# Bias rows in other banks, casts behind copies, keys ahead of low weights: three changes of order in a two-layer decoder trunk

## The chip, the cores and the metric

The kernel runs on one core of a Trainium2 chip. The metric is the device time of one execution in microseconds, the median over several executions. The core's engines run side by side, each through its own queue of instructions: TensorE (PE) multiplies matrices and transposes, VectorE (DVE) and ScalarE (ACT) work element by element, GpSimd (POOL) does little here, and SyncE (SP) issues the loads. An instruction that waits for a semaphore holds everything behind it in its engine's queue.

## The reference

Two layers on a sequence of 256 tokens with 1024 channels. Layer 0 mixes tokens by three groups of dilated causal window attention with a relative bias, layer 1 by gated linear attention (GLA) in chunks of 64. Each is followed by a gated feed-forward network with a short convolution (FFN). Every sub-layer has a norm in front, modulated by shift, scale and gate, which are linear functions of a conditioning vector `c`. The change lies in layer 0's attention:

```
qkv = (h @ w_in).reshape(B, S, 3 groups, 3, 16 heads, 64)
s = einsum(q * 64**-0.5, k) + bias[bucket(distance)]      # per group, masked to the window
p = exp(s - max(s));  o_g = p @ v / sum(p);  lse_g = max(s) + log(sum(p))
o = sum over groups of softmax(lse)_g * o_g
x = x + g1 * (o @ w_out)
```

All inputs are float32. The output is the final norm of `x`.

## The kernel before

**Products.** Each large product is made of three float32r products: a weight tile comes to SBUF as `raw`, ACT casts it to the high part `whi` (line 187, in layer 0's first stage line 412), DVE subtracts to get the low part `wlo` (line 191, there line 417), and PE adds `hi*hi`, `lo*hi` and `hi*lo` (lines 197 to 199 in `mm3`). Activations are split the same way into `hhi` and `hlo`. `raw` has four buffers, `whi` and `wlo` three each. A load can go out when a `raw` buffer is free, which is when its low part has been made.

**Modulation.** The 48 chunks of `w_ada` come through the same `raw` buffers. DVE multiplies them with `c` and sums (line 160), ACT adds the bias (lines 168 and 170). Eight chunks are used in the first stage, one with each of the eight channel tiles (`dots`); the rest go one after each group's queries (`next_ada`) and later.

**Order.** The program is written as a stream; a scheduler orders each engine's instructions by its own estimate of times. `behind(i)` and the arguments `after`, `low` and `late` place instructions in that order behind others. They are no semaphores: waits come from data and from buffers alone.

**Banks.** PSUM has eight banks, in three pools: `p` has two, `s` four, `t` two. `bank(name, tag)` takes the next of a pool; without a tag the pool comes from a fixed cycle, "pstspsts". A bank can be written again when its last reader is done.

**First stage (lines 353 to 447 and 617 to 650).** The squares of `x` are summed on PE into bank `ms`, and ACT makes the norm's factor. Three products with a one-hot matrix (line 374, `rows`) make the bias rows of all heads, ACT copies them to SBUF (line 433), SP stores them to DRAM, and from there each pair of heads loads its bias tile later. Five products on constants (`keep_warm`) follow. Then the eight channel tiles are taken one by one: load the modulation chunk and the weights (`dots`), scale (`scaled`), add the shift and cast (`shifted`), low part (`rest_of`), cast the weights in two pieces (`cast`), low weights (`low`). PE multiplies each tile for the first two of eight head pairs, all of it into eight banks: `s`, `t`, `t`, `p`, `p` and three more `s`.

**Head pairs (lines 652 to 716).** For each further pair `u`: queries and keys of three groups (`queries`, `wqk`, into a `p` bank, evacuated by `evacuate`: ACT's `q` at line 546, DVE's `k` at line 547), values in two halves (`values`, `wv`, into the two `p` banks, copied by ACT in `by_group`), scores (`s` banks), maxima and softmax. The probabilities of the pair before are transposed four tiles at a time (`turn`: PE line 518, ACT's copy to `pt` at line 519) and multiplied with the values (`outputs`: PE lines 526 and 530, then `ohi`, `olo`). The third pair (`u == 2`) is special: two earlier pairs are finished in it. The last (`u == 7`) takes its second half of values after the scores. In `project` the last pair is transposed and finished between the output projection's products.

Of the kernel before, what the change touches and what calls it, by code (L numbers as in the profile page):

```python
# [36 lines left out]
KEYS = T + 2 * CH  # L37
# [20 lines left out]
def trunk(ctx: ExitStack, tc: tile.TileContext, I, out):  # L58
    nc = tc.nc
# [12 lines left out]
    def bank(name="ps", tag=None):  # L72
        tag = tag or next(cycle)
        return psum.tile([P, 512], F32, tag=tag, name=name, bufs={"p": 2, "s": 4, "t": 2}[tag])
# [45 lines left out]
    @contextmanager  # L120
    def behind(*those):

        with ExitStack() as st:
            for i in those:
                st.enter_context(tc.issue_after(i.ins))
            yield

    def keep_warm(n):

        ps = bank("warm")  # L130
        for i in range(n):
            i = mm(ps[:, :P], ones_d, ones_d, start=True, stop=True)
        return i
# [3 lines left out]
    sq = wspl.tile([P, 2048], F32, tag="wlo", name="sq").rearrange("p (k t) -> p k t", k=KT)  # L137
    for n in range(2):
        ps = bank("cb", "t")
# [37 lines left out]
    def split(src, n, dmas=1, after=((), ()), late=(), low=()):  # L177
        raw = wraw.tile([P, 2048], F32, tag="raw", name="raw")
        for i in range(dmas):
            c = slice(n * i // dmas, n * (i + 1) // dmas)  # L180
            last_load[0] = nc.sync.dma_start(raw[:, c], src[:, c])
        hi = wspl.tile([P, 2048], F32R, tag="whi", name="whi")
        lo = wspl.tile([P, 2048], F32R, tag="wlo", name="wlo")
        for i in range(0, n, n // 2):
            c = slice(i, i + n // 2)
            with behind(*after[i > 0]):
                copied[0] = nc.scalar.copy(hi[:, c], raw[:, c])  # L187
        for i in range(0, n, n // 2):
            c = slice(i, i + n // 2)
            with behind(*(late if i else low)):  # L190
                last_lo[0] = nc.vector.tensor_tensor(lo[:, c], raw[:, c], hi[:, c].bitcast(F32), op=ALU.subtract)  # L191
        return hi, lo
# [13 lines left out]
    def rstd_of(squares, n=D, tag=None):  # L206
        ps = bank("ms", tag)
        for i, sq in enumerate(squares):
            a = mm(ps[:, :T], ones_d, sq, start=(i == 0), stop=(i == len(squares) - 1))
        ln = tmp.tile([P, T], F32, tag="ln", name="ln", bufs=2)  # L210
        nc.scalar.activation(ln, ps[:, :T], AF.Ln, bias=eps[:, 0:1], scale=D / n)
        r = tmp.tile([P, T], F32, tag="rstd", name="rstd", bufs=2)
        norm_ops[:] = a, nc.scalar.activation(r, ln, AF.Exp, scale=-0.5)
        return r
# [125 lines left out]
    rows = att.tile([16, NROW], F32, tag="pt", name="rows")  # L340
# [22 lines left out]
    with behind(last_add):  # L363
        on_dve = [scale_terms(0)]
    exp_ln_after(silu)
    r = rstd_of([sq[:, 0, :], sq[:, 4, :]])

    rows_ps, at = [], 0
    with behind(norm_ops[0]):
        for i, (g, n) in enumerate(ROWS):  # L370
            c = slice(at, at + n)
            ps = bank("rows", "tts"[i])[:16, 0:n]
            rows_ps.append((ps, c))
            last_row = mm(ps, tab[:, 16 * g : 16 * g + 16], oh[:33, c], start=True, stop=True)
            at += n
    with behind(last_row):
        warm = keep_warm(5)
# [3 lines left out]
    on_act = [norm_ops[1]]  # L381
# [16 lines left out]
    def shifted(kt):  # L398
        with behind(on_act[0]):
            on_act[0] = nc.scalar.activation(h_hi[kt][:, :], xr[kt], AF.Identity, bias=mod[0, 0, kt][:, 0:1])  # L400

    def rest_of(kt):
        with behind(on_dve[0]):
            on_dve[0] = nc.vector.scalar_tensor_tensor(h_lo[kt][:, :], xr[kt], mod[0, 0, kt][:, 0:1], h_hi[kt][:, :].bitcast(F32),
                                                       op0=ALU.add, op1=ALU.subtract)
        chain[kt] = chain[7] = on_act[0], on_dve[0]
        h.append((h_hi[kt], h_lo[kt]))

    def cast(kt, half):
        c = pieces[half]  # L410
        with behind(on_act[0]):
            on_act[0] = nc.scalar.copy(w0[kt][0][:, c], raw0[kt][:, c])

    def low(kt, half):
        c = pieces[half]
        with behind(on_dve[0]):
            on_dve[0] = nc.vector.tensor_tensor(w0[kt][1][:, c], raw0[kt][:, c], w0[kt][0][:, c].bitcast(F32), op=ALU.subtract)
# [2 lines left out]
    scaled(0)  # L420
    cast(0, 0)
    shifted(0)
    cast(0, 1)
    rest_of(0)
    low(0, 0)
    dots(1)
    low(0, 1)
    scaled(1)
    shifted(1)
    rest_of(1)  # L430
    with behind(on_act[0]):
        for ps, c in rows_ps:
            on_act[0] = nc.scalar.copy(rows[:, c], ps)
    for kt in range(2, KT):
        for half in range(2):
            cast(kt - 1, half)
# [58 lines left out]
    def probabilities(prob, m):  # L495
# [14 lines left out]
                normed_p.append(pn)  # L510
        return normed_p, att.tile([P, 4, KEYS], F32, tag="pt", name="pt")

    def turn(tiles, normed_p, pt):
        for i in tiles:
            t = bank("t", "ttss"[i])
            for j in range(3):
                c = slice(P * j, P * j + P)
                last = nc.tensor.transpose(t[:, c], normed_p[i][:, c], ident)
            nc.scalar.copy(pt[:, i, :], t[:, 0:KEYS])
        return last  # L520

    def outputs(u, v, pt):
# [18 lines left out]
    def evacuate(q, k, g, pq, pk):  # L541

        if g:
            i = nc.scalar.mul(q[g], pq, 0.125)
            return i, nc.vector.tensor_copy(k[g], pk)
        qh, ql = q[0]
        pk = in_order(pk)
        kh, kl = (as_tokens(z[:, 0:T]) for z in k[0])  # L550
        nc.scalar.mul(qh, pq, 0.125)
        i = nc.scalar.copy(kh, pk)
        nc.vector.scalar_tensor_tensor(ql, pq, 0.125, qh.bitcast(F32), op0=ALU.mult, op1=ALU.subtract)
        return i, nc.vector.tensor_tensor(kl, pk, kh.bitcast(F32), op=ALU.subtract)
# [30 lines left out]
        return end  # L585

    def queries(u, g, *qk):
        pq, pk, middle, end = raw_queries(u, g)
        with behind(evacuate(*qk, g, pq, pk)[1]):
            next_ada()  # L590
        return middle, end

    def raw_queries(u, g, tag="p", low=(), by_parts=False):
        w = split(I["wqk"][u - 2, g], 2048, low=low, late=low)
        pqk = bank("pqk", tag)
        pq, pk = pqk[:, :T], pqk[:, T:]
        if by_parts:
            for part in range(3):
                for kt in range(KT):
                    for i, ps in enumerate((pq, pk)):  # L600
                        at = 2 * P * kt + P * i
                        end = mm(ps, w[part == 2][:, at : at + P], h[kt][part == 1], start=(part == kt == i == 0),
                                 stop=(part == 2 and kt == KT - 1 and i == 1))
            return pq, pk, None, end
        for kt in range(KT):
            s, e = kt == 0, kt == KT - 1
            mm3(pq, parts(w, 2 * P * kt), h[kt], s, False)
            end = mm3(pk, parts(w, 2 * P * kt + P), h[kt], False, e)
            if kt == 3:
                middle = end  # L610
        return pq, pk, middle, end
# [13 lines left out]
    pv = b0[3:]  # L625
# [37 lines left out]
    qk = new_qk()  # L663
# [14 lines left out]
    for u in range(2, NPAIR):  # L678
        if u > 2:
            bias = bias_of(u)  # L680
            qk = new_qk()
        with behind(last):
            if u > 2:
                queries(u, 0, *qk)
            middle, end = queries(u, 1, *qk)
        if u == 2:
            bias = bias_of(u)
            with tc.issue_after(last_load[0].ins):
                nc.sync.dma_start(x_all, I["xT"])
        with behind(middle):  # L690
            turn((0, 1), *before)
        with behind(end):
            turned = turn((2, 3), *before)
        if u == 2:
            turned_pt, before = before[1], probabilities(*raised)
        middle, end = queries(u, 2, *qk)
        if u == 2:
            with behind(end):
                outputs(0, v0, turned_pt)
                turn((0, 1), *before)  # L700
        pv = [bank("pv", "p") for _ in range(2)]
        end = values(u, 0, pv)
        if u == 2:
            with behind(end):
                turned = turn((2, 3), *before)
        if u < NPAIR - 1:
            end = values(u, 1, pv)
        with behind(end, turned):
            s, last = scores(*qk)
        with behind(last):  # L710
            last = outputs(u - 1, v, before[1])
        if u == NPAIR - 1:
            with behind(last):
                values(u, 1, pv)
        v = by_groups(pv)
        before = probabilities(*maxima(s, bias))

# [543 lines left out]
```

## Time and profile before

| | us |
|---|---|
| median of 3 runs | 778.48 (778.16 to 780.02) |
| the profiled execution's own time | 778.91 |
| its span, first to last instruction | 777.1 |
| PE busy | 757.8 (98%) |
| DVE busy | 625.5 (80%) |
| ACT busy | 490.7 (63%) |

The granted clock of TensorE was 0.998 over the span. A row of the timeline is: start, duration, engine, line, operation, out<-in, form and count, and in brackets the idle time of that engine just before and what ended it. `SPq` is the load queue. In the waits a row is: engine and work that waited, what it waited for, microseconds in all, times, the longest. Durations of PE's products overlap, so the distance from one start to the next is what a product costs: in the first stage six products of 128x256 take 0.71 us.

### The profile page before, as it was taken

Reading aid. Unit: us, or ns where it says so; the run is one execution under the profiler, and the core shown is the slowest. Engines: PE = TensorE matmul, PEld = TensorE weight load, DVE = VectorE, ACT = ScalarE, POOL = GpSimd, SP = SyncE. Lnnn points to the kernel's source line nnn. Section 1 sums busy time; section 2 is a strip of 40 time slices with the busy share of each in tenths; the row PEclk is TensorE's granted clock in tenths of the full one; section 3 lists DMA queues with packets and bytes.
Section 4 is the critical chain, followed back from the end, with each engine's and each line's share of the span. In section 5 each row is a group of like instructions: output and inputs, shape, how many; then the busy total and the mean of one; then the engine's idle time right before and its main releaser. Section 6 shows DMA issues by size and latency. Waiting matters only on the chain.

```text
span 777.1 us, 15925 instructions
## 1 busy us (share of the span) xinstructions
PE 757.8 (98%) x6420; PEld 731.9 (94%) x6420; DVE 625.5 (80%) x1120; ACT 490.7 (63%) x964; POOL 12.4 (2%) x36
## 2 busy tenths in 40 slices
PE   5999999999999999999999999999999999999997
PEld 2999889999999989999999998898999999999997
DVE  6976978778778868999988778797667998899662
ACT  5555765655666668767666556836667876667552
POOL 0000000000000010000000000000010000000000
PEclk9999999999999999999999999999999999999999
DMA  9987787686886846867646975875245665555641
GB/s 344 400 302 286 214 325 262 226 306 212 311 328 245 313 153 243 278 224 257 233 144 236 341 276 200 324 270 217 84 167 184 219 218 179 202 193 207 242 172 55
DMA packets 36487, 186.29 MB, mean 240 GB/s; under 512 B 8444, under 2 KB 11004, under 8 KB 20286
## 3 DMA queue, kind: packets, MB, share of 16 engines
q1 hardware_dynamic: 36032, 184.84, 66.7%
q8 instruction: 50, 0.82, 0.4%
q10 hardware_dynamic: 382, 0.45, 0.2%
q14 instruction: 23, 0.19, 0.1%
HBM read 184.17 MB, written 1.10 MB: 238 GB/s over the span
## 4 chain that ended last, share of the span: by engine, by line
PE 71%; DMA 13%; DVE 11%; ACT 3%; issue 2%; SPq 0%; DVEq 0%; ACTq 0%
PE pab L199 10%; PE pab L198 10%; PE pab L197 10%; DMA raw<-in_wqk 7%; PE pd L197 5%; PE pd L199 5%; PE pd L198 5%; DVE wlo L191 5%; PE pqk L641 4%; DMA raw<-in_wv 4%; DVE ada_raw L160 2%; PE py L197 2%; PE py L198 2%; PE py L199 2%; ACT whi L187 2%
## 5 line engine op out<-in xcount | busy, mean ns | idle before, releaser
L191 DVE TENSOR_TENSOR wlo<-raw,whi 128x1024 fp32r<-128x1024 f32 (+2 forms) x258 | 273.7, 1094 | 56.6 <-ACT whi L187 55.9
L187 ACT CAST whi<-raw 128x1024 fp32r<-128x1024 f32 (+2 forms) x258 | 230.5, 942 | 115.8 <-PE pab L198 40.7
L199 PE MATMUL pab<-hhi,wlo 128*128 128x256 f32 x672 | 185.1, 277 | 0.0
L198 PE MATMUL pab<-hlo,whi 128*128 128x256 f32 x672 | 185.0, 277 | 0.0
L197 PE MATMUL pab<-hhi,whi 128*128 128x256 f32 x672 | 183.5, 277 | 0.0
L199 PEld LDWEIGHTS pab<-hhi,wlo 128*128 128x128 f32 x672 | 126.3, 188 | 0.0
L198 PEld LDWEIGHTS pab<-hlo,whi 128*128 128x128 f32 x672 | 126.1, 188 | 0.2
L197 PEld LDWEIGHTS pab<-hhi,whi 128*128 128x128 f32 x672 | 125.3, 188 | 0.1
L160 DVE CUSTOM_DVE_ANT_0 ada_raw<-ada_raw,c_bc 128x1024 f32<-128x1024 f32 x96 | 113.6, 1222 | 14.3 <-DMA ada_raw<-in_w_ada 14.3
L198 PE MATMUL pd<-glo,whi 128*128 128x256 f32 x352 | 97.1, 276 | 0.0
L199 PE MATMUL pd<-ghi,wlo 128*128 128x256 f32 x352 | 97.1, 276 | 0.0
L197 PE MATMUL pd<-ghi,whi 128*128 128x256 f32 x352 | 96.8, 276 | 0.0
L197 PE MATMUL pqk<-hhi,whi 128*128 128x256 f32 x328 | 92.4, 282 | 0.0
L199 PE MATMUL pqk<-hhi,wlo 128*128 128x256 f32 x328 | 91.3, 279 | 0.0
L198 PE MATMUL pqk<-hlo,whi 128*128 128x256 f32 x328 | 91.1, 278 | 0.0
L198 PEld LDWEIGHTS pd<-glo,whi 128*128 128x128 f32 x352 | 66.1, 188 | 0.0
L199 PEld LDWEIGHTS pd<-ghi,wlo 128*128 128x128 f32 x352 | 66.1, 188 | 0.0
L197 PEld LDWEIGHTS pd<-ghi,whi 128*128 128x128 f32 x352 | 65.9, 188 | 0.0
L197 PEld LDWEIGHTS pqk<-hhi,whi 128*128 128x128 f32 x328 | 61.8, 188 | 0.5
L199 PEld LDWEIGHTS pqk<-hhi,wlo 128*128 128x128 f32 x328 | 61.7, 188 | 0.3 <-issue 0.3
L198 PEld LDWEIGHTS pqk<-hlo,whi 128*128 128x128 f32 x328 | 61.7, 188 | 0.0
L822 ACT ACTIVATE r<-pab,small 128x256 f32<-128x256 f32 x86 | 46.7, 559 | 15.7 <-DVE r L825 15.6
(226 smaller groups left out, 1389.6 us busy)
## 6 DMA issues: line engine op xcount, KB each, us to landing
ada_raw<-in_w_ada SPq DMA_DIRECT2D x46, 1024.0 KB, 5.8
raw<-in_w_up SPq DMA_DIRECT2D x42, 1024.0 KB, 5.0
raw<-in_w_down SPq DMA_DIRECT2D x32, 704.0 KB, 5.2
raw<-in_wqk SPq DMA_DIRECT2D x18, 1024.0 KB, 7.7
raw<-in_wv SPq DMA_DIRECT2D x14, 768.0 KB, 4.7
raw<-in_w SPq DMA_DIRECT2D x6, 960.0 KB, 5.7
raw<-in_w_out_a SPq DMA_DIRECT2D x4, 1024.0 KB, 7.1
raw<-in_w_v_b SPq DMA_DIRECT2D x4, 1024.0 KB, 5.8
```

Source lines behind the costliest of these rows:

```text
L160: last_dot[0] = nc.vector.tensor_tensor_reduce(w, w, c_bc, op0=ALU.mult, op1=ALU.add, scale=1.0, scalar=0.0, accum_out=dot,)
L187: copied[0] = nc.scalar.copy(hi[:, c], raw[:, c])
L191: last_lo[0] = nc.vector.tensor_tensor(lo[:, c], raw[:, c], hi[:, c].bitcast(F32), op=ALU.subtract)
L197: mm(ps, a[0], b[0], start=start, stop=False)
L198: mm(ps, a[0], b[1], start=False, stop=False)
L199: return mm(ps, a[1], b[0], start=False, stop=stop)
L641: i = mm(ps[j], w[:, at + P * j : at + P * j + P], y, start=s and j % 2 == 0, stop=e and j % 2 == 1)
L822: nc.scalar.activation(r, u[:, :T], AF.Identity, scale=cw[2], bias=col(C_CB + 44 * l + f))
```

## The change

Three parts and what follows from them.

1. *Bias rows.* The three banks of `rows` are taken from `s` instead of `t`, `t`, `s`. ACT copies them behind the first tile's casts, ahead of the second tile's work, instead of behind the second tile's shift. The banks of `keep_warm` and of the first norm come from `p` and no longer from the cycle, so the cycle's later takers get the pool that stands three places before the old one. The first tile's low weights go ahead of its low activations.
2. *Third pair.* The casts of its values' two halves, and of the next pair's first queries, are placed behind copies of transposed tiles (`first`, `second`, `pt_copy`).
3. *Last pair.* The low parts of the second half of its values are placed behind the copy of its last keys (`kept`).

```diff
     def keep_warm(n):
-        ps = bank("warm")
+        ps = bank("warm", "p")
...
-    r = rstd_of([sq[:, 0, :], sq[:, 4, :]])
+    r = rstd_of([sq[:, 0, :], sq[:, 4, :]], tag="p")
...
-            ps = bank("rows", "tts"[i])[:16, 0:n]
+            ps = bank("rows", "s")[:16, 0:n]
...
+    low(0, 0)
+    rest_of(0)
     cast(0, 1)
-    rest_of(0)
-    low(0, 0)
+    with behind(on_act[0]):
+        for ps, c in rows_ps:
+            on_act[0] = nc.scalar.copy(rows[:, c], ps)
     dots(1)
...
-    with behind(on_act[0]):
-        for ps, c in rows_ps:
-            on_act[0] = nc.scalar.copy(rows[:, c], ps)
...
+    pt_copy, kept = [None], [None, None]
...
-            nc.scalar.copy(pt[:, i, :], t[:, 0:KEYS])
+            pt_copy[0] = nc.scalar.copy(pt[:, i, :], t[:, 0:KEYS])
...
-        pq, pk, middle, end = raw_queries(u, g)
-        with behind(evacuate(*qk, g, pq, pk)[1]):
+        pq, pk, middle, end = raw_queries(u, g, after=pt_copy[:1] if (u, g) == (3, 0) else ())
+        kept[:] = evacuate(*qk, g, pq, pk)
+        with behind(kept[1]):
             next_ada()
...
-        w = split(I["wqk"][u - 2, g], 2048, low=low, late=low)
+        w = split(I["wqk"][u - 2, g], 2048, low=low, late=low, after=(after, after))
...
             turned = turn((2, 3), *before)
+        first = pt_copy[:1] if u == 2 else ()
...
                 turn((0, 1), *before)
+        second = pt_copy[:1] if u == 2 else ()
         pv = [bank("pv", "p") for _ in range(2)]
-        end = values(u, 0, pv)
+        end = values(u, 0, pv, after=first)
...
-            end = values(u, 1, pv)
+            end = values(u, 1, pv, after=second)
...
         if u == NPAIR - 1:
             with behind(last):
-                values(u, 1, pv)
+                values(u, 1, pv, low=kept[1:])
```

**Where the rows stand now.** ACT in the first stage, from the first tile's casts on (`hhi` is the cast activation, `mod` a modulation term). Before:

```order
L412 CAST whi<-raw 128x768
L400 ACTIVATE hhi<-xr,mod 128x256
L412 CAST whi<-raw 128x1152
L170 ACTIVATE mod<-dot,small 128x1
L168 ACTIVATE mod<-dot,one_b,small 128x1
L400 ACTIVATE hhi<-xr,mod 128x256
L433 COPY rows<-rows 16x512
L433 COPY rows<-rows 16x128 x2
L412 CAST whi<-raw 128x768
```

Now:

```order
L412 CAST whi<-raw 128x768
L400 ACTIVATE hhi<-xr,mod 128x256
L412 CAST whi<-raw 128x1152
L428 COPY rows<-rows 16x512
L428 COPY rows<-rows 16x128 x2
L170 ACTIVATE mod<-dot,small 128x1
L168 ACTIVATE mod<-dot,one_b,small 128x1
L400 ACTIVATE hhi<-xr,mod 128x256
L412 CAST whi<-raw 128x768
```

The three copies moved ahead of the second tile's modulation terms and activation.

ACT in the third pair, from its middle queries on (`q` is the copy of queries, 768 columns a half of the values, 1024 a half of queries and keys, `ohi` the outputs' high part). Before:

```order
L187 CAST whi<-raw 128x768 x2
L546 ACTIVATE q<-pqk 128x256
L519 COPY pt<-t 128x384 x3
L187 CAST whi<-raw 128x768 x2
L519 COPY pt<-t 128x384
L170 ACTIVATE mod<-dot,small 128x1
L546 ACTIVATE q<-pqk 128x256
L170 ACTIVATE mod<-dot,small 128x1
L187 CAST whi<-raw 128x1024 x2
L535 CAST ohi<-po 128x256
L519 COPY pt<-t 128x384
L170 ACTIVATE mod<-dot,small 128x1 x2
```

Now:

```order
L548 ACTIVATE q<-pqk 128x256
L521 COPY pt<-t 128x384 x4
L187 CAST whi<-raw 128x768 x2
L170 ACTIVATE mod<-dot,small 128x1 x2
L548 ACTIVATE q<-pqk 128x256
L537 CAST ohi<-po 128x256
L521 COPY pt<-t 128x384
L170 ACTIVATE mod<-dot,small 128x1 x2
L521 COPY pt<-t 128x384
L187 CAST whi<-raw 128x768 x2
L521 COPY pt<-t 128x384 x2
L187 CAST whi<-raw 128x1024 x4
```

Both halves of the values are now cast behind transposed tiles, and two pieces of the fourth pair's queries (four casts) stand together behind the last of them.

DVE in the last pair, from the second group's keys on (`k` is the copy of keys, 768 columns a half of the values). Before:

```order
L547 COPY k<-pqk 128x256
L160 ISA ada_raw,dot<-ada_raw,c_bc 128x1024
L160 ISA dot 128x1
L160 ISA ada_raw,dot<-ada_raw,c_bc 128x1024
L160 ISA dot 128x1
L191 TENSOR_TENSOR wlo<-raw,whi 128x768 x2
L547 COPY k<-pqk 128x256
```

Now:

```order
L549 COPY k<-pqk 128x256
L160 ISA ada_raw,dot<-ada_raw,c_bc 128x1024
L160 ISA dot 128x1
L160 ISA ada_raw,dot<-ada_raw,c_bc 128x1024
L160 ISA dot 128x1
L549 COPY k<-pqk 128x256
L160 ISA ada_raw,dot<-ada_raw,c_bc 128x1024
L160 ISA dot 128x1
L160 ISA ada_raw,dot<-ada_raw,c_bc 128x1024
L160 ISA dot 128x1
L191 TENSOR_TENSOR wlo<-raw,whi 128x768 x2
```

The low weights moved behind the last keys and behind one more modulation chunk.

More of the change, by code (lines that the diff above doesn't have):

```diff
@@ L587, in queries, with raw_queries @@
     def queries(u, g, *qk):
-        pq, pk, middle, end = raw_queries(u, g)
-        with behind(evacuate(*qk, g, pq, pk)[1]):
+        pq, pk, middle, end = raw_queries(u, g, after=pt_copy[:1] if (u, g) == (3, 0) else ())
+        kept[:] = evacuate(*qk, g, pq, pk)
+        with behind(kept[1]):
             next_ada()
         return middle, end
-    def raw_queries(u, g, tag="p", low=(), by_parts=False):
-        w = split(I["wqk"][u - 2, g], 2048, low=low, late=low)
+    def raw_queries(u, g, tag="p", low=(), by_parts=False, after=()):
+        w = split(I["wqk"][u - 2, g], 2048, low=low, late=low, after=(after, after))
         pqk = bank("pqk", tag)
```

## The prediction

> **What bounds the kernel now.** I read the page's first part, then the waits of TensorE (PE), then the timelines of PE, ScalarE (ACT), VectorE (DVE) and the load queue (SP) at the three places that the diff touches.
>
> ```profile
> span 777.1 us, 15925 instructions
> ...
> PE 757.8 (98%) x6420; PEld 731.9 (94%) x6420; DVE 625.5 (80%) x1120; ACT 490.7 (63%) x964; POOL 12.4 (2%) x36
> ```
>
> PE is busy for 98% of the span: 777.1 - 757.8 = 19.3 us of idle time is all that a change of order can win. The list of PE's waits says where it lies (columns: total us, times, longest).
>
> ```profile
> PE warm L132 <- ACT rows L433: 6.4, 1, 6.4
> PE pv L197 <- DVE k L547: 1.4, 1, 1.4
> PE po L526 <- ACT pt L519: 1.3, 1, 1.3
> ...
> PE pv L198 <- DVE wlo L191: 0.6, 1, 0.6
> ...
> PE s L470 <- ACT pt L519: 0.2, 1, 0.2
> ```
>
> The first is the bias rows, the second the last pair's keys, and those that name `pt` (a third one of them, 0.4 us, is quoted below) the third pair. No row names the FFN's banks (`pab`, `pd`).
>
> **The bias rows.** Timeline of the start:
>
> ```profile
> 10.00 2.74 PE L374 MATMUL rows<-oh,tab 33*16 33x512 f32 x6
> ...
> 12.62 1.14 ACT L412 CAST whi<-raw 128x1152 fp32r<-128x1152 f32 x1
> ...
> 15.28 0.29 ACT L170 ACTIVATE mod<-dot,small 128x1 f32<-128x1 f32 x1 [1.52 <-DVE dot L160]
> ...
> 18.51 0.87 ACT L433 COPY rows<-rows 16x512 f32<-16x512 f32 x3
> ...
> 19.12 2.50 PE L132 MATMUL warm<-ones_d 128*128 128x128 f32 x10 [6.38 <-ACT rows L433]
> 19.29 1.88 ACT L412 CAST whi<-raw 128x768 fp32r<-128x768 f32 x2
> ...
> 21.27 0.77 PE L641 MATMUL pqk<-hhi,whi 128*128 128x256 f32 x2
> ```
>
> The five warm-up products take a `t` bank that still holds bias rows; all of PE's queue stands behind them until ACT has copied those rows out, behind tile 1's activation. Now the rows lie in `s` banks, the warm-up in a `p` bank, and nothing of ACT stands before it: it can start at 12.74 (10.00 + 2.74) instead of 19.12, and the first layer's products at 21.27 - 6.38 = 14.9. What they then need is there: the second cast ends at 13.76, and the row copies behind it at 13.76 + 0.87 = 14.6. Those copies cost ACT nothing, as they lie in the 1.52 us in which ACT waited at 15.28; without that cover, 0.87 us of tile 1's chain. They also leave the place ahead of tile 1's casts, which can start at about 18.5 instead of 19.29. The exchange of `low(0, 0)` and `rest_of(0)` on DVE moves instructions that PE needs only after 14.9: nothing.
>
> But PE cannot keep all of it, because casts of later tiles come at their old times. The last tile (kt = 7) decides:
>
> ```profile
> 51.08 1.87 ACT L412 CAST whi<-raw 128x768 fp32r<-128x768 f32 x2
> ...
> 57.81 0.87 PE L641 MATMUL pqk<-hhi,whi 128*128 128x256 f32 x6
> 58.52 0.51 PE L637 MATMUL pqk<-whi,hhi 128*128 128x384 f32 x2
> ...
> 64.16 2.05 PE L602 MATMUL pqk<-hhi,whi 128*128 128x256 f32 x16
> ...
> 40.00:50.00 10.00, 10.00 (x81) 10.00 (x81) 9.10 (x15) 5.09 (x9) 0.00 (x0) 1.00 1.01 392
> ```
>
> (The last row is a window of the stage: after its times PE, weight load, DVE, ACT and GpSimd busy, clock, share of the DMA engines, GB/s.) The DMA engines are full here, so supply is not moved. Tile 7's second cast ends at 51.08 + 1.87 = 52.95; the product that reads it starts at 58.52. PE may come 58.52 - 52.95 = 5.57 us earlier and no more. **I take -5.5.** Upper end 6.38, if the casts come earlier too; lower end 0, in the rival of supply below.
>
> Does the gain survive the next loads?
>
> ```profile
> 63.62 0.60 SPq L353 DMA_DIRECT2D bias<-rows_d  x1
> 67.15 0.33 SPq L181 DMA_DIRECT2D raw<-in_wqk  x1
> ...
> 72.02 2.00 ACT L187 CAST whi<-raw 128x1024 fp32r<-128x1024 f32 x2 [0.40 <-DMA raw<-in_wqk]
> ...
> 81.50 0.38 PE L197 MATMUL pqk<-hhi,whi 128*128 128x256 f32 x1
> ```
>
> The load at 67.15 is the first that frees with PE's progress, but in the queue it stands behind the bias rows' loads, which end at 63.62 + 0.60 = 64.2 whatever PE does. It moves by 2.9 us only, its cast to about 69.1, ending at 71.1; PE wants it at 81.5 - 5.5 = 76. Cover of 4.9 us, so nothing is lost. Later loads wait for buffers that DVE frees behind PE's own results, so they move with PE.
>
> **The third pair.** (Times as before the change; all shift by -5.5.)
>
> ```profile
> 93.85 0.33 PE L197 MATMUL pv<-whi,hhi 128*128 128x384 f32 x1
> 94.02 0.34 PE L198 MATMUL pv<-wlo,hhi 128*128 128x384 f32 x1
> ...
> 96.52 1.08 PE L526 MATMUL po<-pt,v 128*64 128x256 f32 x8 [1.29 <-ACT pt L519]
> ...
> 98.00 0.55 PE L518 MATMUL t<-ident,pn 128*128 128x128 f32 x3
> ...
> 103.32 0.66 PE L518 MATMUL t<-ident,pn 128*128 128x128 f32 x4 [0.41 <-ACT pt L519]
> ```
>
> ```profile
> 94.52 1.56 ACT L187 CAST whi<-raw 128x768 fp32r<-128x768 f32 x2 [1.32 <-DMA raw<-in_wv]
> 96.00 0.47 ACT L519 COPY pt<-t 128x384 f32<-128x384 f32 x1
> ...
> 105.61 2.00 ACT L187 CAST whi<-raw 128x1024 fp32r<-128x1024 f32 x2 [1.60 <-DMA raw<-in_wqk]
> ...
> 95.87 1.82 DVE L191 TENSOR_TENSOR wlo<-raw,whi 128x768 fp32r<-128x768 f32 x2
> ...
> 97.72 0.33 SPq L181 DMA_DIRECT2D raw<-in_wqk  x1
> ...
> 111.07 0.38 PE L197 MATMUL pqk<-hhi,whi 128*128 128x256 f32 x1
> ```
>
> A `pt` copy stands in ACT's queue behind a cast that waits 1.32 us for its load. With casts behind copies these three waits go: 1.29 + 0.41 + 0.2 (the third from the list) = 1.9 us. But the second half's value weights (cast at 94.52) are now cast only behind the copy of the second transposed tile of the next pair. In the new order PE does 23 value products between the first tile's transposes and that second one. From 93.85, where the query products ended: outputs 1.5 (96.52 to 98.00), three transposes 0.3, 23 products at 0.17 (93.85 to 94.02) 3.9, three transposes 0.3: 99.9. Then the copy 0.4, a cast half 0.8 (of 1.56) and a low half 0.9 (of 1.82): 102.0. PE, after one product and six transposes (0.8), stands at that place at 100.7 and needs the low half with its second product. So about 1.2 of the 1.9 us comes back as a wait for `wlo`. Four 1 us casts then stand ahead of the copies of `v`, which free the bank for the fourth pair's queries; the last load among them, issued at 97.72 and cast at 105.61, moves late with its buffer and may hold the bank back some 0.2 us. **I take -0.5**: -1.9 + 1.2 + 0.2. From -1.9 (no new wait) to +2 (that load 4 us late and both waits kept away, -1.9 + 3.9).
>
> **The last pair.**
>
> ```profile
> 248.03 1.57 ACT L187 CAST whi<-raw 128x768 fp32r<-128x768 f32 x2 [1.24 <-DMA raw<-in_wv]
> ...
> 249.98 0.36 ACT L546 ACTIVATE q<-pqk 128x256 f32<-128x256 f32 x1
> ...
> 248.90 1.83 DVE L191 TENSOR_TENSOR wlo<-raw,whi 128x768 fp32r<-128x768 f32 x2 [0.33 <-ACT whi L187]
> 250.65 0.42 DVE L547 COPY k<-pqk 128x256 f32<-128x256 f32 x1
> ...
> 251.12 0.45 PE L197 MATMUL pv<-whi,hhi 128*128 128x384 f32 x1 [1.45 <-DVE k L547]
> ...
> 256.42 0.44 PE L197 MATMUL pv<-whi,hhi 128*128 128x384 f32 x1
> ```
>
> PE waits for the bank that holds queries and keys; the keys' copy stands behind 1.83 us of low weights, and goes ahead. Yet the same bank waits for ACT's `q` copy, whose place is kept: behind the cast that waits for a load, it ends at 249.98 + 0.36 = 250.34. The keys' copy ended at 251.07, and PE ran at 251.12. So 251.07 - 250.34 = 0.73 us goes and the rest of the 1.45 stays, with `q` as its new releaser. **I take -0.7**; from 0 to -1.45. The low weights, now behind the keys and 2.4 us of modulation products as well, end near 253 and are for the products at 256.42. The last transposes come later in PE's order, eight products of the output projection ahead of the outputs, for one copy of 0.47 (as at 96.00): nothing, at worst those 0.5.
>
> **Banks of later stages.** The rotation "pstspsts" now starts three places earlier. Each bank comes back after eight takings in either phase, and no FFN bank is in the list of waits: nothing; one bad hand-over would cost about what the small waits cost, 0.2 to 0.6.
>
> **Sum:** -5.5 - 0.5 - 0.7 = -6.7. The profiled execution took 778.91 us (span 777.1 and 1.8 around it), 0.43 above the median of 778.48. It would take 772.2, and the median becomes **771.8**.
>
> **Rivals.**
> *Supply holds the first stage (same):* products start early and then wait tile by tile, and the stage ends where it did. For it: DMA share 1.01, DVE busy for 9.1 us of 10. Against it: the 5.57 us between tile 7's cast and its product. The time would be 778.48 - 0.5 - 0.7 = 777.3. The Trainium skill ("DMA: Bandwidth & Descriptors", Specifications) puts a core's limit to HBM at about 358 GB/s; by that, as an estimate, the 40 us of loads at 392 GB/s would take 9.5% or 3.8 us longer, which leaves 1.8 of the 5.57 us. The window's 392 GB/s is above that figure, so the trace decides against it. Chance 0.08.
> *Loads erode it:* only the 2.9 us by which the first freed load can move survives, and later pairs wait: 778.48 - 2.9 - 1.2 = 774.4. For it: the queue behind the bias loads, and the 0.6 us wait for `wlo` in the waits' list, which says that supply is nearly late even now. Against it: the 4.9 us of cover. Chance 0.14.
> *All named waits go:* 6.38 + 1.9 + 1.45 = 9.7, so 768.8, if casts and loads move too. Chance 0.10.
> *Slower:* the casts of the third pair, now late, free raw buffers late; the weights of 105.61 wait for a load that starts after them, the copies of `v` stand behind their cast on ACT, and PE's fourth pair waits for the bank. PE comes there at 111.07, or 110.4 with what the pair wins; less 2.0 for the cast and about 1.3 for four copies of `v` (an estimate: three `pt` copies as at 96.00) it needs the load by 107, and each us after that passes to PE in full. A buffer freed by the low half's end at about 103 and the same 7.9 us of load (97.72 to 105.61) make 111, 4 us late and still faster than before. The point from which it decides is a landing at 107 + 5.5 + 0.7 + 1.9 - 1.2 = 114, 16 us after the old issue: two loads queued before it instead of one. One load more (7.9) is 119 and 778.5 + 5 = 783. Chance 0.04.
>
> **How the numbers follow.** Forecast 0.64, its own range 770.3 to 773.7 (the likeliest less the third pair's other 1.4, plus 1.9 of its 2.5). Erosion and the cleared waits widen the 8-in-10 range to 768.9 to 775.6. A measurement here tells changes above 0.3%, 2.3 us. Faster: forecast, erosion (4.1 us) and cleared waits, 0.88; within: 0.08; slower: 0.04.
>
> **What will show it.** Right: no wait of the warm-up for the row copies; products from about 15 us; a wait of PE for a cast near 52 us, and L602's successor row at about 58.6; a `wlo` wait in place of `pt` waits near 95; a 0.7 us wait for `q` in the last pair. Wrong: first stage ending after 60 us, PE waiting for the second wqk load near 76, or new waits in pairs four to seven.

## The result, and the profile after

The changed kernel takes 773.37 us (median of 8 runs, 769.98 to 776.47) beside 778.32 of the kernel before (8 runs, 776.44 to 780.65). The ratio is 0.9932, 95% interval 0.9907 to 0.9956: 3.4 to 7.2 us faster. A second set of runs of the same kernel, told below, gave 0.992 (0.989 to 0.995). The forecast of 771.8 was in its range, its -6.7 us a little large.

Landmarks of three executions, each the start of a PE row in the timeline:

| us | before | after | after, second profile |
|---|---|---|---|
| first products | 21.27 | 14.78 | 14.89 |
| first row behind the first stage | 64.16 | 59.45 | 59.21 |
| queries of the fourth pair | 111.07 | 104.91 | 104.66 |
| first transposes of the last pair's turn | 240.66 | 234.16 | 235.23 |
| `pd` of the first FFN | 408.84 | 402.05 | 403.08 |
| `ms` behind the first `pr` | 540.96 | 532.52 | 533.72 |
| last output rows | 770.64 | 761.73 | 762.93 |
| the execution | 778.91 | 769.98 | 771.18 |

So 4.7 us are won in the first stage, 1.5 up to the fourth pair, another 0.6 up to the first FFN's `pd`, and then 1.7 us at the first `pr`, which have another cause (last section). Without these the first pair of profiles differs by some 7.2 us. Both profiled executions of the changed kernel were the fastest of their set of runs, so they show more gain than the median does.

The waits of PE after, from 0.5 us up (to be held against the list of before):

```profile
PE pv L197 <- DVE k L549: 1.3, 1, 1.3
PE warm L132 <- DVE eps L105: 1.2, 1, 1.2
PE pv L198 <- DVE wlo L191: 0.9, 2, 0.5
PE pr L199 <- DVE wlo L191: 0.9, 1, 0.9
...
PE pv L197 <- ACT whi L187: 0.5, 1, 0.5
```

The 6.4 us for `rows` and the three waits for `pt` are gone; a `whi` wait and a second `wlo` wait are new; the wait for `k` in the last pair is nearly as long as before.

PE in the first stage after (the first rows, then the last tile), and ACT at the same two places:

```profile
12.63 2.50 PE L132 MATMUL warm<-ones_d 128*128 128x128 f32 x10
14.78 1.63 PE L644 MATMUL pqk<-hhi,whi 128*128 128x256 f32 x6
16.21 0.52 PE L640 MATMUL pqk<-whi,hhi 128*128 128x384 f32 x1
16.53 1.48 PE L644 MATMUL pqk<-hhi,whi 128*128 128x256 f32 x6
...
51.70 0.87 PE L644 MATMUL pqk<-hhi,wlo 128*128 128x256 f32 x6
52.65 0.97 PE L644 MATMUL pqk<-hhi,whi 128*128 128x256 f32 x6
53.70 0.63 PE L640 MATMUL pqk<-whi,hhi 128*128 128x384 f32 x2
...
59.45 2.05 PE L605 MATMUL pqk<-hhi,whi 128*128 128x256 f32 x16
```

```profile
12.59 1.14 ACT L412 CAST whi<-raw 128x1152 fp32r<-128x1152 f32 x1
13.63 0.89 ACT L428 COPY rows<-rows 16x512 f32<-16x512 f32 x3
14.84 0.29 ACT L170 ACTIVATE mod<-dot,small 128x1 f32<-128x1 f32 x1 [0.32 <-DVE dot L160]
...
51.78 1.87 ACT L412 CAST whi<-raw 128x768 fp32r<-128x768 f32 x2
```

The row copies lie where the prediction put them, in time in which ACT waited. The last tile's second cast ends at 51.78 + 1.87 = 53.65, and the product that reads it starts at 53.70: the 5.57 us between the two are used up. No bracket says so, but the distances do: six products from 51.70 to 52.65 and six from 52.65 to 53.70 take 0.95 and 1.05 us instead of 0.71, so PE waited some 0.6 us for that tile.

The third pair after, PE and then ACT:

```profile
95.60 0.82 PE L520 MATMUL t<-ident,pn 128*128 128x128 f32 x6
96.88 0.61 PE L197 MATMUL pv<-whi,hhi 128*128 128x384 f32 x2 [0.47 <-ACT whi L187]
97.88 0.45 PE L198 MATMUL pv<-wlo,hhi 128*128 128x384 f32 x1 [0.38 <-DVE wlo L191]
```

```profile
95.62 0.48 ACT L521 COPY pt<-t 128x384 f32<-128x384 f32 x1 [2.18 <-PE t L520]
95.99 1.57 ACT L187 CAST whi<-raw 128x768 fp32r<-128x768 f32 x2
```

Three waits of 1.94 us in sum have become two of 0.85: the cast starts behind the copy, as intended, and PE waits for its first half and then for the low half made of it.

The last pair after, DVE and then ACT:

```profile
243.99 0.42 DVE L549 COPY k<-pqk 128x256 f32<-128x256 f32 x1 [1.43 <-ACT q L548]
```

```profile
241.65 1.57 ACT L187 CAST whi<-raw 128x768 fp32r<-128x768 f32 x2 [0.86 <-DMA raw<-in_wv]
...
243.60 0.36 ACT L548 ACTIVATE q<-pqk 128x256 f32<-128x256 f32 x1
```

DVE is free now, and waits: the copy of `k` starts when that of `q` has ended (243.60 + 0.36 = 243.96). That was hidden before behind the low weights.

### The profile page after: what moved, and what is told of

Same layout as the page of the kernel before. It is cut to its first block, busy times and chain, and to the rows that moved or that the text cites. A ratio compares the mean times of both kernels' runs of the same rounds, so it can differ in the third digit from the quotient of the medians.

```text
span 768.2 us, 15928 instructions
## 1 busy us (share of the span) xinstructions
PE 756.4 (98%) x6420; PEld 730.1 (95%) x6420; DVE 625.2 (81%) x1120; ACT 490.3 (64%) x964; POOL 12.3 (2%) x36
## 4 chain that ended last, share of the span: by engine, by line
PE 68%; DMA 13%; DVE 13%; ACT 3%; issue 2%; SPq 0%; ACTq 0%; DVEq 0%
PE pab L199 10%; PE pab L197 10%; PE pab L198 10%; DMA raw<-in_wqk 6%; PE pd L197 5%; PE pd L199 5%; PE pd L198 5%; DVE wlo L191 5%; DMA ada_raw<-in_w_ada 4%; DMA raw<-in_wv 3%; DVE ada_raw L160 3%; PE py L197 2%; PE py L198 2%; PE py L199 2%; PE pv L197 2%
```

## The experiments

**The three parts alone.** First the bias rows without the other two (the diff without its parts 2 and 3).

> Bias rows in the `s` banks, their copies early, and the warm-up bank in the new place; third and last pair are as before. Theory (the start pays, but the first products run at half rate, 0.24 us apart, until about 18.8 us): no wait of the warm-up, first products at about 14.8, first stage ends (layer 1's first value products, L602 of the kernel before) near 59.5 instead of 64.16, and the landmarks stay about 4.7 us early from there on: 773.6 us by the median. Rival (supply holds the later stages, or the scheduler's other order of the third and last pair takes part back): early at 59.5, but no more than 3 us early at the fourth pair's queries (111.07 before): 775.5 or more.

Measured: 774.94 us, ratio 0.9967 (0.9945 to 0.9988). Products at 14.78, first stage done at 59.63, but fourth pair's queries at 107.44, 3.6 us early and no longer 4.5 as at the end of the first stage. PE's waits in this kernel:

```profile
PE po L528 <- ACT pt L521: 1.8, 1, 1.8
PE pqk L197 <- ACT v L566: 1.4, 1, 1.4
...
PE pqk L644 <- ACT whi L412: 0.6, 1, 0.6
```

Early PE meets the third pair's loads in the old order: it waits longer for `pt`, and then for the bank that the `v` copies free, the very place of the prediction's slower rival. The median stands between theory and rival.

*The third pair's part alone, twice:*

```diff
+        first = pt_copy[:1] if u == 2 else ()
...
+        second = pt_copy[:1] if u == 2 else ()
...
-        end = values(u, 0, pv)
+        end = values(u, 0, pv, after=first)
```

(with the same for the second half and for the fourth pair's first queries).

> Casts of the third pair behind the copies of transposed tiles; start and last pair are as before. Theory (from the profile after: three `pt` waits of 1.94 us in sum become waits of 0.47 for `whi` and 0.38 for `wlo`): fourth pair's queries at about 110.0 instead of 111.07, and 777.2 us. Rival (what the prediction had): the `wlo` wait comes back with about 1.2 us, 0.2 us more at the bank of `v`, fourth pair's queries at about 110.6, 777.8 us. Second rival (the gain came only since the start runs earlier in the full change): not earlier than 111.0, 778.3 us.

> The third pair's part alone a second time, for a second profile. The first look took 782.66 us: its loads of the first stage moved 330 to 350 GB/s between 30 and 50 us (before: 382 to 392), the load of the third pair's queries was 3.7 us late, and PE waited 2.85 us for normalized probabilities. Theory (that is chance of the one execution, common to all these kernels): with loads as in the profile before, fourth pair's queries at about 109.6 instead of 111.07, no wait above 0.5 us before them, and the new median lies below the one of before by 1 us or more. Rival (the part alone makes the third pair wait for its loads): the wait near 90 us is there again though the loads come on time, and the time is that of before or above.

Measured: 778.16 us, ratio 1.001 (0.9991 to 1.0029), and 776.59, ratio 0.9976 (0.9955 to 0.9998). In both profiles the two waits for `whi` and `wlo` are those of the full change (0.47 and 0.38) and no `pt` wait is left, but ahead of them stands a new one, here that of the first:

```profile
90.78 0.87 PE L520 MATMUL t<-ident,pn 128*128 128x128 f32 x3 [2.85 <-DVE pn L508]
```

Fourth pair's queries came at 114.30 and 113.20. In both the first stage's loads were late: the last tile's second cast ended at 55.46 and 55.77 (before: 52.95). So the second profile could not test the theory as written. What the part is worth alone stays open; the two medians, each against the kernel before in its own set of runs (777.50 and 778.37), put it between +0.7 and -1.8 us.

*The last pair's part alone:*

```diff
-                values(u, 1, pv)
+                values(u, 1, pv, low=kept[1:])
```

> Keys of the last pair copied ahead of the low weights; start and third pair are as before. Theory (the keys' copy also waits for the queries' copy on ScalarE, which stands behind a cast that waits for its load): the wait of 1.45 us for `k` in the last pair stays at 1.2 to 1.4, a gain of 0.1 to 0.2 us, 778.2 us. Rival (the prediction): 0.7 us of it goes and the rest names `q`, 777.6 us.

Measured: 778.28 us, ratio 1.0008 (0.9992 to 1.0023). The wait for `k` there is 1.13 us (before 1.45), 0.32 shorter: nearer to the theory's 0.1 to 0.2 than to the rival's 0.7.

*The whole change without the last pair's part:*

> The whole change without the last pair's part. Theory (the third pair's part is worth 2 us or more once the start is early, since the start alone met waits of 1.8 us for `pt` and 1.4 us for the bank of `v` there; the last pair's part is worth 0.2 us): fourth pair's queries at about 104.9 as with the whole change, the wait for `k` in the last pair at about 1.5, and 773.5 us. Rival (the last pair's part brings a good part of the gain by moving the transposes and projections behind it): 1 us or more slower than the whole change, 774.5 us.

Measured: 774.42 us, ratio 0.9951 (0.9927 to 0.9976). Fourth pair's queries at 104.08, 7.0 us early, against 3.6 with the bias rows alone; 1.3 of these 3.4 us are its first stage, done at 58.35, so the third pair's part is worth 2.1 us once the start is early. The wait for `k` is 1.74. The whole change measured in the same set of runs was 772.71, so the two medians differ by 1.7 us: more than the wait explains, with intervals that overlap. In this profile the stretch from the fourth pair to the last took 3.8 us longer than in the kernel before, through the fifth pair, for a reason that other profiles show too (below), so the difference says nothing certain on the last pair.

*The changed kernel once more:*

> The changed kernel once more, for a second profile beside the others of this call. Theory (executions differ by how fast the loads of the first 50 us come and by whether TensorE's clock drops after a wait of 0.9 us): median near 773.4 us, and this profile differs from the first at those two places only. Rival (something else differs): the landmarks drift apart elsewhere.

Measured: 772.71 us, ratio 0.992 (0.989 to 0.995). Up to the fourth pair the two profiles differ by 0.25 us, in pairs four to seven by 1.3 us: a wait of 0.40 for `k` at 176.68, 0.64 instead of 0.55 for `wlo` at 185.31, and gaps too short for the list. This is the rival's drift, in the middle pairs; and the theory's two places don't suffice.

**Who ends the first stage now?** The five warm-up products left out:

```diff
-        warm = keep_warm(5)
+        warm = last_row
```

> The changed kernel without the five warm-up products, so that the first products may start at about 13.8 instead of 14.8 us. Theory (the end of the first stage is now set by the casts of the last tiles, that is by the loads): PE waits for a cast near 40 to 53 us, and the stage ends at 59.0 to 59.5 as with the change, no gain: 773.4 us. Rival (the half rate of the first products, until 18.8 us, is what cost the stage 1.8 us): the products still start 1 us earlier at half rate, the stage ends 0.5 us earlier, 772.9; or, if the warm-up is what raises the clock, the half rate lasts longer and it ends later, 774 or more.

Measured: 773.15 us, ratio 0.9927 (0.9899 to 0.9954), no gain over the change. The first products start at 12.71, 2.1 us earlier than with the change, and run at half rate until 16.5; with the warm-up that lasts until 16.4 to 18.6 (last section), so it ends no later without the warm-up. PE and ACT at the last tile of this kernel:

```profile
52.64 0.62 PE L640 MATMUL pqk<-whi,hhi 128*128 128x384 f32 x2
```

```profile
50.70 1.89 ACT L412 CAST whi<-raw 128x768 fp32r<-128x768 f32 x2
```

Cast done at 52.59, product at 52.64, stage done at 58.38. The stage's end follows the cast, not the start: cast to end is 5.79 here, 5.80 after, 5.80 and 5.83 in the two partial kernels above; it was 11.2 before. The stage ends 1.1 us before that of the first profile after, earlier than the theory had it, because the cast came so much earlier in this execution; the kernel without the last pair's part, which has the warm-up, ended its stage at 58.35 with a cast at 52.55. The half rate of the first products, the rival's cause, costs little that PE would not wait for anyway: where the cast came at 53.33 (second profile after), PE reached it 0.24 us later.

*The banks as changed, but the row copies where the kernel before has them:*

```diff
-    with behind(on_act[0]):
-        for ps, c in rows_ps:
-            on_act[0] = nc.scalar.copy(rows[:, c], ps)
     dots(1)
...
+    with behind(on_act[0]):
+        for ps, c in rows_ps:
+            on_act[0] = nc.scalar.copy(rows[:, c], ps)
```

> The changed kernel with the copies of the bias rows (and the order of the first tile's low parts) where the kernel before has them, behind tile 1's activation; the banks stay as in the change. Theory (the banks alone let the warm-up and the first tile's products into the `t` banks start, but the products into the `s` banks, where the rows now lie, must wait for the copies): warm-up at 12.6, first products at about 14.8, then a wait of some 2 us for `rows` until about 19.3, and the first stage ends near 59.5 to 60, as the last tiles' casts decide; about 773.5 us. Rival (the early copies carry the gain): the first stage ends 1.5 us or more later than with the change, 775 us.

Measured (one run): 773.48 us. PE:

```profile
14.75 1.57 PE L644 MATMUL pqk<-hhi,whi 128*128 128x256 f32 x6
16.16 0.51 PE L640 MATMUL pqk<-whi,hhi 128*128 128x384 f32 x2
19.06 1.25 PE L644 MATMUL pqk<-hhi,whi 128*128 128x256 f32 x6 [2.39 <-ACT rows L433]
...
61.90 2.05 PE L605 MATMUL pqk<-hhi,whi 128*128 128x256 f32 x16
```

The wait only moved to the `s` banks, and the stage ends at 61.90, 7.4 us behind its last cast (52.59 + 1.88): PE sets the end again. Against the first profile after, early copies are worth 2.45 us of the 4.7 there; the rival is right on the stage. That the whole run is no slower than the changed kernel's median says little, being one run: from its fourth pair's queries (108.37) to the last pair's turn it took 129.25 us, as short as in the first profile after and shorter than in any other.

*Extra transfers, that nothing waits for,* ahead of the last tiles' loads (16 instead of 8 in the second kernel):

```diff
+        if kt == 3:
+            spare = dram.tile([P, 8 * T], F32, name="spare")
+            for i in range(8):
+                nc.gpsimd.dma_start(spare[:, T * i : T * i + T], h_hi[kt][:, :].bitcast(F32))
```

> The changed kernel with 1 MB of extra transfers put into the first stage (eight times a tile of 128 KB from SBUF to a spare place in HBM, from the GpSimd queue, once the fourth tile's activations are there): nothing waits for them, they only take the DMA engines' time, by the 390 GB/s of the windows some 2.7 us. Theory (the cover of the loads behind the start is spent, since the last tiles' casts already come 0.2 us ahead of their products): the first stage ends 2 to 2.7 us later than 59.45, and the fourth pair's queries and the later landmarks are late by as much or more, 775.5 to 777 us. Rival (the prediction's cover of 4.9 us behind the start is there): at most 0.5 us later at the fourth pair's queries (104.9), and no more than 773.5.

> The same with 2 MB of extra transfers, some 5.4 us of the DMA engines' time. Theory (no cover left): 4.5 us or more later than the changed kernel at the fourth pair's queries, about the whole gain of the start lost, 778 us. Rival (a cover of 4.9 us): 0.5 to 1 us later there, 774 us.

> The kernel before with the same 1 MB of extra transfers in its first stage (the scheduler places some instructions otherwise from the third pair on, so its first stage compares best). Theory (its casts came 5.57 us ahead of their products, so it has the cover that the changed kernel has spent): no wait of PE for a cast in the first stage, layer 1's first scores at 69.8 to 70.4 as without the transfers (changed kernel: 65.2 without, 68.4 with them); behind that the loads of the third pair are some 2.7 us late and cost up to 2 us: 778 to 780 us. Rival (the transfers hurt TensorE's work in another way than through the casts): the first scores come 2 us or more later than 69.9.

Measured:

| | changed | changed + 1 MB | changed + 2 MB | before | before + 1 MB |
|---|---|---|---|---|---|
| last tile's second cast ends, us | 53.65 | 56.71 | 58.34 | 52.95 | 55.50 |
| first stage ends | 59.45 | 62.71 | 64.13 | 64.16 | 64.47 |
| fourth pair's queries | 104.91 | 108.98 | 109.58 | 111.07 | 112.55 |
| median | 773.37 | 778.08 | 777.72 | 778.32 | 778.66 |
| ratio to the kernel before | 0.9932 | 0.9998 (0.998 to 1.0016) | 0.9998 (0.998 to 1.0017) | | 1.0016 (0.9997 to 1.0035) |

PE's wait for a cast in the changed kernel with 1 MB, the last tile of the changed kernel with 2 MB (PE, then ACT), and the last cast of the kernel before with 1 MB, where PE waits for no cast of the first stage:

```profile
PE pqk L648 <- ACT whi L412: 1.5, 1, 1.5
```

```profile
57.33 0.96 PE L648 MATMUL pqk<-hhi,whi 128*128 128x256 f32 x6 [0.24 <-ACT whi L412]
58.39 0.62 PE L644 MATMUL pqk<-whi,hhi 128*128 128x384 f32 x2
...
64.13 2.05 PE L609 MATMUL pqk<-hhi,whi 128*128 128x256 f32 x16
```

```profile
56.46 1.88 ACT L412 CAST whi<-raw 128x768 fp32r<-128x768 f32 x2
```

```profile
53.62 1.88 ACT L412 CAST whi<-raw 128x768 fp32r<-128x768 f32 x2
```

The same megabyte costs the kernel before 0.3 us of its first stage and the changed one 3.3, and in the median 1.3 us (its own set of runs has the kernel before at 777.39) against 4.7. The medians say less than the stage, since the kernel before with 1 MB has another order of instructions from the third pair on; the changed kernel's order is the same with and without the transfers. The theory holds: the cover of the kernel before is what the change has turned into time, and there is none left. With 2 MB this is plainest: the last cast is done at 58.34, the product that reads it starts at 58.39, and the stage ends 5.79 us behind the cast, as without the transfers. With 1 MB a part is the clock: after the wait of 1.53 us it fell to 0.59 and 0.55 between 44 and 48 us, which cost some 1.6 us, and PE came to the last tile 0.30 us behind its cast (57.01 and 56.71). In the first stage with 2 MB it fell nowhere, and behind the first stage the 2 MB cost no further time.

**The last pair's wait.** The whole change, and the casts of the second half behind the queries' copy:

```diff
-                values(u, 1, pv, low=kept[1:])
+                values(u, 1, pv, after=kept[:1], low=kept[1:])
```

> The whole change, and in addition the casts of the last pair's second half of value weights stand behind the queries' copy on ScalarE. Theory (that cast, waiting for its load, held the queries' copy, and the keys' copy waited for that): the wait of 1.3 us for `k` near 244.5 falls to 0.4 or less, and the time is about 1 us under the changed kernel's, 772.3 by its median, if the cast's own products, some 5 us later, still find it. Rival (the copies are late for another cause, the end of the products that they read): the wait stays above 1 us, and no gain. Second rival: the late cast now makes PE wait for `whi` or `wlo` in the last pair by as much as was won.

Measured: 772.63 us, ratio 0.9939 (0.9915 to 0.9962), the changed kernel's time. The wait for `k` is 1.08 us, with 0.48 at the first half besides. ACT:

```profile
240.67 1.57 ACT L187 CAST whi<-raw 128x768 fp32r<-128x768 f32 x2 [2.71 <-DMA raw<-in_wv]
242.15 0.38 ACT L548 ACTIVATE q<-pqk 128x256 f32<-128x256 f32 x1
...
246.02 0.39 ACT L168 ACTIVATE mod<-dot,one_b,small 128x1 f32<-128x1 f32 x1 [0.85 <-DVE dot L160]
246.32 0.36 ACT L548 ACTIVATE q<-pqk 128x256 f32<-128x256 f32 x1
```

The cast is out of the way, but a modulation term stands there, which waits for DVE, and DVE is late since the first half's cast waited 2.71 us for its load. The theory falls in its size: with one instruction taken from ahead of `q`, the next one held it.

## Why the prediction was right, and where it was off

**Bias rows, -5.5.** Measured -4.7. The mechanism is as predicted, with the cap at the last tile's second cast. The term is 0.8 too large since that cast ended at 53.65 and no longer 52.95 (0.70) and the products behind it took 0.11 longer. It is no fixed number: in six executions of kernels with the early start (without extra transfers or late copies) the cast ended between 52.55 and 53.80 and the stage between 58.35 and 59.63, so the term is -4.5 to -5.8 against the profile before. Here the prediction's reading "supply is not moved" is what became the bound.

**Cover of the next loads, nothing lost.** Right in what it concluded for the first of them: the second `wqk` cast, now at 70.35, ended at 72.4, and PE took up those queries at 76.80 without a wait. The load itself moved by 2.0 us and not by 2.9 (from 67.15 to 65.16): the bias rows' loads ahead of it did not end at 64.2 but at 65.1. The step failed in the sentence on later loads, that they "move with PE". From the fourth pair's queries to the last pair's turn the kernel before took 129.59 us, the changed one 129.25 and 130.57, and three kernels that were as early at the fourth pair 131.61 (casts behind the queries' copy), 133.35 (without the last pair's part) and 133.03 (without the warm-up). The second of these shows how:

```profile
155.80 0.44 PE L197 MATMUL pv<-whi,hhi 128*128 128x384 f32 x1 [1.14 <-ACT whi L187]
156.79 0.65 PE L198 MATMUL pv<-wlo,hhi 128*128 128x384 f32 x1 [0.55 <-DVE wlo L191]
```

```profile
154.91 1.57 ACT L187 CAST whi<-raw 128x768 fp32r<-128x768 f32 x2 [2.35 <-DMA raw<-in_wv]
```

The load of the fifth pair's second half of values lands late for PE. These three kernels have the same order of instructions as the changed one up to the last pair (but for the warm-up), so it is the execution that differs: the rival "loads erode it" is at work in some executions and not in others. The three that lost time there took 773.5 to 773.7 us as a whole, near the medians; the two of the changed kernel that lost next to none took 769.98 and 771.18. That fits this loss being most of what stands between the profiles' 7.2 us and the median's 5.0, but the other executions have no profile, so it isn't shown.

That PE is 7 us early is not what it takes. From its own queries to the next pair's, the fifth pair took 29.2 us in all four profiles of kernels without the third pair's part, 29.2 to 29.6 in four with it, and 31.6 to 34.4 in six with it. One of these six is the third pair's part alone (second profile), whose fourth pair began at 113.20, later than before. There and in the three kernels above, the weights of the fourth pair's last queries began to be cast 3.7 to 4.0 us behind that pair's first product; in the first profile after it was 2.2 (107.10), in the kernel before 0.5 (111.56). So the loads were late before the fifth pair began. New waits in pairs four to seven were among the prediction's signs of being wrong, and these executions have them. Whether the third pair's late casts, as the slower rival has it, or only the loads' rate in these executions is the cause was not separated. In the profile above, some 1.4 us of the loss are also the clock, which fell behind the wait of 1.14 us.

**Third pair, -0.5.** Measured -1.5 in the two profiles (6.16 less 4.70). All three `pt` waits went, as predicted; what came back was 0.85 us and not 1.2, in part since PE has two products with the cast ahead of the first that reads the low half, and not one. The 0.2 us for the bank of `v` didn't come. The other 0.4 us are gaps too short for the list. The part's value depends on the start: alone it can't be told from nothing, behind an early start it is worth 2.1 us. The slower rival's wait for that bank didn't come either: with the whole change the fourth pair found it free.

**Last pair, -0.7.** Measured -0.2 (1.45 to 1.29), -0.3 (the part alone) and -0.4 (the second profile after). The step that failed: "0.73 us goes" took the end of `q` for the end of the wait. The copy of `k` starts only when that of `q` has ended and takes 0.42 us itself. In all eight profiles with this order it starts 0.39 or 0.40 us behind the start of `q`, and in the five without it (leaving out the kernel before with 1 MB) 0.66 or 0.67: 0.28 us is what the order wins. The wait itself also depends on when `q` comes; with the early start it was 1.80 and 1.74 us without this part, so against those two profiles the wait fell by more, 0.45 to 0.8. That `q` would be named as the releaser was right, on DVE's row and not on PE's.

**Banks of later stages, 0.** Right: none is in the list of waits. From the rows `early` ahead of the first FFN to its `pd` the changed kernel takes 121.8 us and 122.3 in its two profiles, the kernel before 122.2.

**The sum.** Start 0.8 too much, third pair 1.0 too little, last pair 0.5 too much: -6.4 by the landmarks, near the -6.7 forecast. That the sum came so near is luck, as the errors of the terms offset each other. The medians differ by 5.0 us.

## What to carry to other kernels

When a start is pulled forward, look for the instruction whose input comes at its own time, and take its distance to its reader as the gain; from there on the loads are the bound, and every later microsecond of them counts in full. Parts that repair orders further on may be worth nothing alone and much behind the part that makes the engine early, so judge them on top of it. Before moving a copy ahead of its neighbour, see what the copy itself waits for when the neighbour is gone.

## What the runs showed of the hardware

**A short wait can halve the clock for microseconds, or not.** Both kernels wait 0.9 us for `wlo` at the first `pr`. Windows around it (columns as in the prediction; the clock is the third number from the end), before and after:

```profile
534.00:536.00 2.00, 2.00 (x11) 2.00 (x12) 2.00 (x2) 2.00 (x3) 0.00 (x0) 0.60 0.51 115
536.00:538.00 2.00, 2.00 (x12) 2.00 (x11) 2.00 (x3) 0.60 (x2) 0.00 (x0) 0.55 0.99 414
```

```profile
526.00:528.00 2.00, 1.07 (x9) 0.87 (x9) 2.00 (x2) 2.00 (x6) 0.00 (x0) 1.00 0.01 4
528.00:530.00 2.00, 2.00 (x20) 2.00 (x19) 2.00 (x3) 1.88 (x3) 0.00 (x0) 1.00 0.99 274
```

Before, the products behind the wait are 0.21 us apart for 3.3 us, after 0.11: 1.7 us that are no part of the change. The same fall came behind waits of 1.14 (0.72 and 0.50 in the kernel without the last pair's part), 1.53, 1.8, 1.82 and 2.85 us, and stayed away behind others of 0.9 to 2.0. The Trainium skill ("TensorE: Matmul & The Clock Gate", Part 1: The HAM clock gate) has the clock fall after an idle window of some 3.4 us. Here waits of 0.91 to 2.85 us were enough at times. The same section of the Trainium skill says that the window runs free of the kernel, which would make it a matter of chance; the runs agree with that, but don't show the window.

**The first products run at half rate under a clock column of 1.00.** They start 0.21 us apart instead of 0.12 (with a longer step behind the first, six take from 14.78 to 16.21), until 16.4 to 18.6 us in executions whose code is the same up to there.

**The loads' rate differs between executions.** From 30 to 50 us the same first stage moved 382 and 392 GB/s (two windows of 10 us) in the kernel before and 330 and 350 in the first profile of the third pair's part alone, with the last cast 2.5 us later. The first stage of the kernel before doesn't feel that (it ends at 64.0 to 64.7 us in five executions); that of the changed one does.
